# Output projection by seven block products, with weight differences made inside the mLSTM heads

## The chip, the cores and the metric

The kernel runs on one core of a Trainium2 chip. The metric is the device time of one execution in microseconds (us), lower is better. The core has a matrix engine (PE, with its weight loads listed as PEld), a vector engine (DVE), an engine for functions of single elements (ACT), a general one (POOL), and an engine that here only issues transfers between memory and on-chip buffers (SP). Each works through its own instructions in order.

## What is computed

A block with two branches, an mLSTM with four heads and an S5 scan, over x of 1024 rows and 1024 columns in fp32. The branches are merged with gates g, and the merged rows go through one output projection, a norm and a sum with x:

```python
xn = rmsnorm(h, norm_pre_g[l])
proj = xn @ w_in[l]
...
y_a = mlstm_branch(...) @ w_a_out[l]
y_b = s5_branch(...) @ w_b_out[l]
g = jax.nn.sigmoid(g_pre.astype(jnp.float32)).astype(h.dtype)
merged = g[..., :D_MODEL] * y_a + g[..., D_MODEL:] * y_b
h = h + rmsnorm(merged @ w_o[l], norm_post_g[l])
```

`merged`, `w_o` and the product of the two are all 1024x1024. The change is in the last line.

## The kernel before

Every fp32 product is made from three faster ones. A value is split into a high part in the type fp32r and the rest, its low part; `dot3` (L181 to L184) issues high by high (L182), and the two mixed products (L183, L184). So one output bank of 128x512 over k blocks of 128 takes 3k matmuls. Weights come raw into tiles `wr` (two buffers), ACT copies them into `wh` (L142), and DVE or POOL subtracts to give `wl` (L144).

The schedule is written by hand: `tc.manual_schedule()` keeps the order of the code on each engine. The weights stand in a queue filled by `plan`; `fetch` loads the next one (all loads and stores are issued on SP's queue), `pump` splits one and then puts another `fetch` on the list `pending`, `take` hands it to the user. Work comes in units: `run` first empties `pending` (`tick`: this is where stores and fetches reach SP), then does the unit's own loads, then the unit, then those parts of earlier units that were put off by `defer`. `fill` runs the next unit from the list `fillers`.

After the S5 branch and the projections come the four heads. Inside head h stand the attention's own steps (`attn_a` to `attn_e`) and, between them, units of other work: in the first three heads the projections of the next head (`u_unit`, `o_unit`, `z_unit`, `k_unit`, `v_unit`), in the last head the units of the product with `w_a_out` (`ya_unit`), whose weights are loaded in pieces of 256 columns, `("ya", i)`. `o_unit` writes its gate through a tile `sow` with two buffers to scratch memory `so_d` (ACT at L902). `attn_e` splits a head's result: ACT makes the high part, POOL the low part (L1270), and both are stored to `yh_d` and `yl_d`. `ya_unit` stores partial merged rows to `pa_d`, and `ya_pre` loads what it needs, `y_gb<-gb_d` among it (L1296). `load_so` is L1133, all stores by `store` are L82.

The last stage has three kinds of units. `ya_unit(3, ...)`: four of 18 matmuls. `mg_unit(ct, hf)`: sixteen of 6 matmuls of 512 columns, which complete the merged rows ct (of 128) of one half hf of the sequence, in two DVE operations, and split them into `mh` (ACT, L1439) and, one unit later, `ml` (POOL, L1440). `wo_unit(i, t)`: for each of four pieces of 256 columns of `w_o` and each of eight tiles of 128 rows, 24 matmuls of 256 columns into one bank; ACT squares the bank and sums it for the norm (L1460), DVE multiplies it by the gain (L505 under the name ob). With the last piece come the root (POOL, L1467 and L1468), the sum with x (DVE, L1474) and the store.

## Time and profile before

| | |
|---|---|
| three runs | 989.7, 990.56, 987.15 us, median 989.7 |
| the profiled execution | 987.63 us, of which its span is 985.9 |
| PE busy | 972.8 us, 99% of the span, 5644 matmuls |
| DVE, ACT, POOL busy | 621.9 (63%), 352.9 (36%), 207.1 us (21%) |
| granted PE clock, mean | 0.999 of full speed |
| transfers | 145.17 MB, 147 GB/s over the span |

The span is what the trace covers, and the profiled execution's time is 1.7 us longer. Busy time counts an engine's instructions, on PE with pipelined ends that are modelled. An engine that is idle costs nothing by itself: what counts is what PE, or whoever comes last, waits for. In the rows below a timeline's row gives start, duration, engine, line, operation, output and input; "x2" is two instructions in a row, and brackets give the idle time before the row and what ended it.

### The profile page before, as it was taken

Reading aid. Unit: us, or ns where it says so; the run is one execution under the profiler, and the core shown is the slowest. Engines: PE = TensorE matmul, PEld = TensorE weight load, DVE = VectorE, ACT = ScalarE, POOL = GpSimd, SP = SyncE. Lnnn points to the kernel's source line nnn. Section 1 sums busy time; section 2 is a strip of 40 time slices with the busy share of each in tenths; the row PEclk is TensorE's granted clock in tenths of the full one; section 3 lists DMA queues with packets and bytes.
Section 4 is the critical chain, followed back from the end, with each engine's and each line's share of the span. In section 5 each row is a group of like instructions: output and inputs, shape, how many; then the busy total and the mean of one; then the engine's idle time right before and its main releaser. Section 6 shows DMA issues by size and latency. Waiting matters only on the chain.

```text
span 985.9 us, 15233 instructions
## 1 busy us (share of the span) xinstructions
PE 972.8 (99%) x5644; PEld 840.9 (85%) x5644; DVE 621.9 (63%) x1397; ACT 352.9 (36%) x697; POOL 207.1 (21%) x215
## 2 busy tenths in 40 slices
PE   9999999999999999999999999998999999999997
PEld 7888888888887889978998898888988888879997
DVE  5437968879644752444686677747775888664225
ACT  7413132231314421224544445434543452233211
POOL 3013122111112000013111321223222311462002
PEclk9999999999999999999999999999999999999999
DMA  7454323423434566115344254335437895772504
GB/s 257 109 159 150 96 89 99 111 57 110 110 97 166 186 216 229 59 68 148 97 134 152 82 178 124 134 97 177 133 117 226 281 302 191 243 249 90 193 1 172
DMA packets 113722, 145.17 MB, mean 147 GB/s; under 512 B 18888, under 2 KB 71280, under 8 KB 113648
## 3 DMA queue, kind: packets, MB, share of 16 engines
q1 hardware_dynamic: 113648, 144.21, 46.0%
q8 instruction: 44, 0.72, 0.3%
q14 instruction: 30, 0.25, 0.1%
HBM read 98.79 MB, written 45.38 MB: 146 GB/s over the span
## 4 chain that ended last, share of the span: by engine, by line
PE 88%; issue 3%; POOL 3%; DVE 2%; DMA 2%; ACT 1%; SPq 0%; DVEq 0%; POOLq 0%; ACTq 0%
PE pp L182 24%; PE pp L183 23%; PE pp L184 23%; PE pm L184 4%; PE pm L182 4%; PE pm L183 4%; PE pm L1151 1%; POOL wl L144 1%; PE pm L727 1%; PE pm L768 1%; PE pm L767 1%; PE pm L1074 1%; DMA so_d<-sow 1%; POOL ml L1440 1%; POOL t2k L1270 1%
## 5 line engine op out<-in xcount | busy, mean ns | idle before, releaser
L182 PE MATMUL pp<-xh,wh 128*128 128x512 f32 x768 | 306.9, 400 | 0.0
L183 PE MATMUL pp<-xl,wh 128*128 128x512 f32 x768 | 303.8, 396 | 0.0
L184 PE MATMUL pp<-xh,wl 128*128 128x512 f32 x768 | 303.8, 396 | 0.0
L182 PEld LDWEIGHTS pp<-xh,wh 128*128 128x128 f32 x768 | 144.4, 188 | 35.1 <-ACT wt L691 0.8
L184 PEld LDWEIGHTS pp<-xh,wl 128*128 128x128 f32 x768 | 144.4, 188 | 34.6
L183 PEld LDWEIGHTS pp<-xl,wh 128*128 128x128 f32 x768 | 144.5, 188 | 32.4 <-DVE xl L295 0.3
L144 POOL TENSOR_TENSOR wl<-wr,wh 128x1024 fp32r<-128x1024 f32 (+1 forms) x25 | 61.6, 2482 | 229.1 <-ACT wh L142 229.1
L142 ACT ACTIVATE wh<-wr 128x1024 fp32r<-128x1024 f32 (+2 forms) x74 | 71.0, 1006 | 46.5 <-PE pm L183 30.6
L184 PE MATMUL pp<-wh,ml 128*128 128x256 f32 x256 | 72.6, 284 | 1.3 <-POOL ml L1440 1.3
L144 DVE TENSOR_TENSOR wl<-wr,wh 128x1024 fp32r<-128x1024 f32 (+2 forms) x49 | 55.9, 1172 | 27.7 <-ACT wh L142 23.2
L182 PE MATMUL pp<-wh,xh 128*128 128x256 f32 (+1 forms) x256 | 72.3, 282 | 0.6 <-ACT sow L902 0.6
L183 PE MATMUL pp<-wl,mh 128*128 128x256 f32 x256 | 72.5, 283 | 0.0
L182 PE MATMUL pp<-wh,mh 128*128 128x256 f32 x256 | 71.9, 281 | 0.0
L184 PE MATMUL pp<-wh,xl 128*128 128x256 f32 (+1 forms) x256 | 71.8, 281 | 0.0
L183 PE MATMUL pp<-wl,xh 128*128 128x256 f32 (+1 forms) x256 | 71.8, 280 | 0.0
L308 ACT ACTIVATE tg<-pp 128x512 f32<-128x512 f32 x32 | 19.2, 598 | 127.4 <-PE pp L184 89.4
L1048 POOL TENSOR_TENSOR hll<-t2k,hlh 128x512 fp32r<-128x512 f32 x16 | 21.1, 1319 | 182.7 <-ACT hlh L1047 106.0
L184 PEld LDWEIGHTS pp<-wh,ml 128*128 128x128 f32 x256 | 48.1, 188 | 1.7 <-POOL ml L1440 1.7
L182 PEld LDWEIGHTS pp<-wh,mh 128*128 128x128 f32 x256 | 48.7, 190 | 0.5 <-ACT mh L1439 0.4
L182 PEld LDWEIGHTS pp<-wh,xh 128*128 128x128 f32 x256 | 48.1, 188 | 1.2 <-ACT sow L902 1.0
L183 PEld LDWEIGHTS pp<-wl,xh 128*128 128x128 f32 x256 | 48.2, 188 | 0.2
L184 PEld LDWEIGHTS pp<-wh,xl 128*128 128x128 f32 x256 | 48.1, 188 | 0.0
(412 smaller groups left out, 1810.0 us busy)
## 6 DMA issues: line engine op xcount, KB each, us to landing
wr<-in_w_in_dram SPq DMA_DIRECT2D x48, 512.0 KB
t_d<-tg SPq DMA_DIRECT2D x32, 256.0 KB
xt<-in_x_dram SPq DMA_DIRECT2D x8, 512.0 KB
aux<-t_d SPq DMA_DIRECT2D x16, 256.0 KB
gb_d<-aux SPq DMA_DIRECT2D x16, 256.0 KB
so_d<-sow SPq DMA_DIRECT2D x32, 128.0 KB
sz_d<-t2k SPq DMA_DIRECT2D x16, 256.0 KB
cs_d<-t2k SPq DMA_DIRECT2D x16, 256.0 KB
```

The lines of the kernel that those rows point to most:

```text
L142: A.activation(hi, raw, AF.Copy)
L144: eng.tensor_tensor(wl[:, k0:k0 + n, c0:c0 + w], raw, hi.bitcast(F32), op=ALU.subtract)
L182: PE.matmul(o, lh, rh, start=first, stop=False)
L183: PE.matmul(o, lh, rl, start=False, stop=False)
L184: PE.matmul(o, ll, rh, start=False, stop=last)
L308: A.activation(t, o, AF.Tanh, scale=0.5)
L727: PE.matmul(o[NS * b2:NS * (b2 + 1), g * P:(g + 1) * P], q["wt"][:, ri, g, NS * b2:NS * (b2 + 1)], ut[b][:, 2 * g + b2, :], start=True, st ...
L767: PE.matmul(o, m0[:, 2 * g + b2, :], ut[b][:, 2 * g + b2, :], start=True, stop=False)
L768: PE.matmul(o, vs[:, b2, g].rearrange("p t n -> p (t n)"), ss_[:, b2, g, :], start=False, stop=True)
L1048: PL.tensor_tensor(lo, acc, hi.bitcast(F32), op=ALU.subtract)
L1074: PE.matmul(pm[:, 256 * k:256 * k + 256], wt[:, e, 256 + P * k:256 + P * k + P], wt[:, e, 0:256], start=e == 0, stop=e == 1)
L1151: PE.matmul(sc[:, :P], k_[:, m, sl], q_[:, m, sl], start=m == 0, stop=m == 1)
```

## The change

The 1024x1024 product is cut into four blocks of 512 on either side, and made from seven block products instead of eight (in Winograd's form of Strassen's scheme). With A the merged rows and B the weights `w_o`, each product is a sum or difference of A's blocks by a sum or difference of B's:

- p1 = a11 by b11, p2 = a12 by b21, p3 = s4 by b22, p4 = a22 by one combination of the b's, p5 = s1, p6 = s2 and p7 = s3 by three more;
- c11 = p1 + p2, u2 = p1 + p6, u4 = u2 + p5, c22 = u4 + p7, c21 = u2 + p7 + p4, c12 = u4 + p3.

Each product is four units, one bank of 128x512 each, of 4 blocks of k by three matmuls of 512 columns; the last unit of p3 is done in two halves of 256 columns.

**Weights.** The three differences and the fourth combination don't depend on the data, but are made on the chip: `wo_steps`, called in the last `u_unit` of each of the four heads' projections, loads two tiles `wc` with pieces of the four blocks of `w_o` (into the buffers of `wr`), has POOL make four subtractions of 128x256 in each, one and two units later, and four units later stores both to scratch memory `wt_d`. From the call to the stores the list `held` keeps `fetch` from loading the next weights. In the last stage the queue of weights has p1, p2, p6, p5, p7, p4, p3, each 512x512.

**Merged rows and sums.** The low parts are now made by DVE (`al`). When both rows of a pair of the second half are there, `s_pair` makes s3 and s2 by DVE and s1 by POOL; s4 follows later, and the sums are split by ACT and DVE or POOL (`split_1`). The units of ya and mg stand in another order, and the last six mg units stand among those of p1 and p2.

**Ends.** DVE adds each bank to the running sum, ACT squares it, POOL multiplies by the gain (`pmul`), the root is taken on POOL after a DVE sum, and `finish` adds x as before.

Three places of the order are shown. On SP's queue, in the fourth call of `wo_steps`, which comes at the end of the third head; wr is a weight tile of `w_a_out`, xh and xl the rows of y read back, so and y_gb tiles for the head and for ya units. Before:

```order
L1285 DMA xh_97<-yh_d 128x512
L1286 DMA xl_105<-yl_d 128x512
L124 DMA wr<-in_w_a_out_dram 128x4x256
L124 DMA wr<-in_w_a_out_dram 128x2x256
L1133 DMA so<-so_d 128x256 x2
L1294 DMA y_t_7760<-t_d 128x512
L1296 DMA y_gb<-gb_d 128x512
```

and in the changed kernel some 25 transfers later on that queue:

```order
L1336 DMA y_gb<-gb_d 128x512
L1173 DMA so<-so_d 128x256
L83 DMA pa_d<-y_gb 128x512
L1035 DMA wt_d<-wc 128x2x256 x4
L125 DMA wr<-in_w_a_out_dram 128x4x256
L125 DMA wr<-in_w_a_out_dram 128x2x256
L1334 DMA y_t_8113<-t_d 128x512
L1336 DMA y_gb<-gb_d 128x512
L125 DMA wr<-in_w_a_out_dram 128x4x256
L125 DMA wr<-in_w_a_out_dram 128x2x256
```

The load of the second ya piece, which stood ahead of the head's first loads of so, now stands behind the third store of pa_d and the four stores of wt_d, and the third piece's load follows two transfers after it.

On POOL, in the third call, around the low parts of the head's result (L1270 before, L1310 after). Before:

```order
L144 TENSOR_TENSOR wl<-wr,wh 128x1024
L1098 MEMSET vh 128x4
L1099 MEMSET vh 128x4
L1100 MEMSET vl 128x4x2
L1270 TENSOR_TENSOR t2k<-t2k 128x512 x2
L1048 TENSOR_TENSOR hll<-t2k,hlh 128x512
L1050 TENSOR_SCALAR t2k<-t2k,par 128x512
```

and after:

```order
L1140 MEMSET vl 128x4x2
L1026 TENSOR_TENSOR wc<-wc 128x256 x4
L1310 TENSOR_TENSOR t2k<-t2k 128x512 x2
L1026 TENSOR_TENSOR wc<-wc 128x256 x4
L1088 TENSOR_TENSOR hll<-t2k,hlh 128x512
L1090 TENSOR_SCALAR t2k<-t2k,par 128x512
```

Four subtractions of the weights stand ahead of the two of the head's result, and four behind.

On DVE, in the last stage, where the mg units of the second half end. Before (ft and fpa are the rows of mg units, ob those of the output):

```order
L1432 SCALAR_TENSOR_TENSOR ft<-ft,pp 128x512
L505 TENSOR_TENSOR ft<-ft,fpa 128x512
L505 TENSOR_TENSOR ob_9040<-pp,gpo 128x256
L144 TENSOR_TENSOR wl<-wr,wh 128x1024 x2
L505 TENSOR_TENSOR ob_9081<-pp,gpo 128x256
```

and after (r_8701 and r_8702 are rows of the second half and the sums made from them, s2l the low part of s2, a22l that of the block a22, c the sums c11):

```order
L1500 SCALAR_TENSOR_TENSOR r_8702<-r_8702,pp 128x512
L511 TENSOR_TENSOR r_8702<-r_8702,fpa 128x512
L511 TENSOR_TENSOR c_9087<-m_8949,pm 128x512
L511 TENSOR_TENSOR a22l<-r_8702,a22h 128x512
L511 TENSOR_TENSOR r_8701<-r_8693,r_8701 128x512
L511 TENSOR_TENSOR r_8702<-r_8702,r_8701 128x512
L145 TENSOR_TENSOR wl<-wr,wh 128x1024
L511 TENSOR_TENSOR c_9088<-m_8949,pm 128x512
L1520 TENSOR_TENSOR s2l_8886<-r_8702,s2h_8884 128x512
```

Between an mg unit's two operations and the weights for the next product stand the low part, the two differences of the pair and a sum of the output; one half of those weights is DVE's, the other POOL's.

The diff, without the lines that are removed from the last stage and without those helpers of it that the words above describe:

```diff
+    held = []
+
     def fetch():
-        if order and not raw_q:
+        if order and not raw_q and not held:
...
-    for i in range(4):
-        plan(("wo", i), [w_o[0][:, 256 * i:256 * i + 256]], KT, 256)
+    wo11, wo12 = w_o[0][0:512, 0:512], w_o[0][0:512, 512:1024]
+    wo21, wo22 = w_o[0][512:1024, 0:512], w_o[0][512:1024, 512:1024]
+    for n, src in (("p1", wo11), ("p2", wo21), ("p6", wt_d[1, 1]), ("p5", wt_d[0, 0]), ("p7", wt_d[0, 1]),
+                   ("p4", wt_d[1, 0]), ("p3", wo22)):
+        plan(n, [src], 4, 512)
...
+    wsteps = deque((j, q) for j in range(4) for q in range(2))
+
+    def wo_load():
+        j, q = wsteps.popleft()
+        t = wp.tile([P, 2, 2, DH], F32, tag="wr", name="wc")
+        rows = w_o[0].rearrange("(a j p) c -> j p a c", a=2, j=4)[j]
+        for a in range(2):
+            SY.dma_start(t[:, a], rows[:, a].rearrange("p (b c) -> p b c", b=2)[:, :, DH * q:DH * q + DH])
+        return j, q, t
+
+    def wo_comb(j, q, t):
+        sub_ = lambda o, a, b: PL.tensor_tensor(o, a, b, op=ALU.subtract)
+        b11, b12, b21, b22 = t[:, 0, 0], t[:, 0, 1], t[:, 1, 0], t[:, 1, 1]
+        sub_(b11, b12, b11)
+        sub_(b12, b22, b12)
+        sub_(b22, b22, b11)
+        sub_(b21, b21, b22)
+
+    def wo_store(j, q, t):
+        for a in range(2):
+            SY.dma_start(wt_d[a][:, P * j:P * j + P, DH * q:DH * q + DH].rearrange("b p c -> p b c"), t[:, a])
+
+    def wo_steps():
+
+        held.append(1)
+        ts_ = []
+        pending.append(lambda: ts_.extend(wo_load() for _ in range(2)))
+        defer(lambda: wo_comb(*ts_[0]))
+        defer(lambda: wo_comb(*ts_[1]), 2)
+        defer(lambda: pending.extend([lambda: [wo_store(*t) for t in ts_], held.pop, fetch]), 4)
...
         if m and hf:
             pump(pl=True)
+            wo_steps()
...
+            A.activation(ah[b][:, j], t1, AF.Copy)
+            defer(lambda: tt(al[b][:, j], t1, ah[b][:, j].bitcast(F32), ALU.subtract))
+        if hf:
+            pair.setdefault(j, []).append(ct)
+            if len(pair[j]) == 2:
+                defer(lambda: s_pair(j))
...
+    def split_1(n, j, src, eng):
+        h_, l_ = sv[n][0][j], sv[n][1][j]
+        A.activation(h_, src, AF.Copy)
+        return lambda: eng.tensor_tensor(l_, src, h_.bitcast(F32), op=ALU.subtract)
+
+    def s_pair(j):
+
+        a11, a12, a21, a22 = mrow(j, 0), mrow(4 + j, 0), mrow(j, 1), mrow(4 + j, 1)
+        tt(a21, a11, a21, ALU.subtract)
+        tt(a22, a22, a21, ALU.subtract)
+        PL.tensor_tensor(a11, a11, a22, op=ALU.add)
+        defer(split_1(2, j, a22, V))
+        for n, r in ((1, a11), (3, a21), (4, a12)):
+            late_s[n].append((j, r))
+
+    def split_s(n, eng, cnt=1):
+        for j, r in late_s[n][:cnt]:
+            if n == 4:
+                PL.tensor_tensor(r, r, mrow(4 + j, 1), op=ALU.subtract)
+            split_1(n, j, r, eng)()
+        del late_s[n][:cnt]
...
+    def mul_unit(w, lhs, o, tq, cs=slice(0, 512)):
+        hi, lo = lhs
+        sl = slice(tq * P, (tq + 1) * P)
+        for k in range(4):
+            dot3(o, hi[k][:, sl], lo[k][:, sl], *wcur[w](k, cs), k, k == 0, k == 3)
...
+    def wset2():
+
+        fetch()
+        key, _, _, raws = raw_q.popleft()
+        assert key == "p2"
+        h_ = [main.tile([P, 2, 512], F32R, tag=f"xh{4 + k}", name=f"w2h{k}") for k in range(2)]
+        l_ = [main.tile([P, 2, 512], F32R, tag=f"xl{4 + k}", name=f"w2l{k}") for k in range(2)]
+        for i in range(2):
+            raw = raws[i][2]
+            A.activation(h_[i], raw, AF.Copy)
+            PL.tensor_tensor(l_[i], raw, h_[i].bitcast(F32), op=ALU.subtract)
+        wcur[2] = lambda k, cs: (h_[k // 2][:, k % 2, cs], l_[k // 2][:, k % 2, cs])
+        pending.append(fetch)
...
+    def p2(q):
+        if q == 0:
+            c11 = [main.tile([P, 2, 512], F32, tag=f"xh{6 + i}", name=f"c11{i}") for i in range(2)]
+            cb_[0] = [c11[i // 2][:, i % 2] for i in range(4)]
+            hl1 = [block("a1", "s1h", F32R), block("a2", "s1l", F32R)]
+            sv[1] = [rows4(a) for a in hl1]
+        o = mbank()
+        mul_unit(2, (rows4(ah[1]), rows4(al[1])), o, q)
+        tt(cb_[0][q], cb_["m1"][:, q], o, ALU.add)
+        square(cb_[0][q], q, 0)
+        if q == 1:
+            cb_["g"] = main.tile([P, D], F32, tag="xl6", name="gpo")
+            store(cb_["g"], norm_post_g[0].partition_broadcast(P))
+        if q > 1:
+            split_s(1, PL)
+
+    def p6(q):
+        if q == 0:
+            wset(6)
+            cb_["u2"] = block("a3", "u2")
+            y_space(4, 4)
+        o = mbank()
+        mul_unit(6, sv[2], o, q)
+        tt(cb_["u2"][:, q], cb_["m1"][:, q], o, ALU.add)
+        if q == 0:
+            pump()
+        if q < 2:
+            split_s(1, PL)
+        split_s(3, V)
...
+    def p3(q):
+        if q == 0:
+            cb_[1] = rows4(block("a7", "c12"))
+            cb_["raw"] = block("a6", "c12r")
+        n = 1 if q < 3 else 2
+        w = 512 // n
+        o = mbank()
+
+        for i in range(n):
+            cs = slice(w * i, w * i + w)
+            mul_unit(3, sv[4], o[:, cs], q, cs)
+            r = cb_["raw"][:, q, cs]
+            tt(r, cb_["u4"][:, q, cs], o[:, cs], ALU.add)
+            square(r, q, 1 + i)
+            dst = cb_[1][q][:, cs]
+            if n == 1:
+                pmul(dst, r, 512)
+            else:
+                mul(dst, r, cb_["g"][:, 512 + w * i:512 + w * i + w])
+            if i < n - 1:
+                step2()
+                tt(sso[:, q, 3:4], sso[:, q, 3:4], sso[:, q, 1:2], ALU.add)
+        if q < 3:
+            ending(q, n)
+        else:
+            finish(q, rms(q, n))
...
+    def go(f, q):
+        run(unit(lambda: f(q)))
+
+    go(p1, 0)
+    fill(2)
+    for q in range(1, 4):
+        go(p1, q)
+        fill(1)
+        if q == 1:
+            wset2()
+    go(p2, 0)
+    fill(1)
+    go(p2, 1)
+    pump(pl=True)
+    for f, q in [(p2, q) for q in range(2, 4)] + [(f, q) for f in (p6, p5, p7, p4, p3) for q in range(4)]:
+        go(f, q)
+    flush2()
     tick()
 
 

```

## Rows read from the trace of the kernel before

**Rows 1.** The page, part 1: busy us, share of span, instructions by engine.

```profile
PE 972.8 (99%) x5644; PEld 840.9 (85%) x5644; DVE 621.9 (63%) x1397; ACT 352.9 (36%) x697; POOL 207.1 (21%) x215
```

**Rows 2.** Timeline of PE: start us, duration us, engine, line, operation, count.

```profile
99.81 0.39 PE L182 MATMUL pp<-xh,wh 128*128 128x512 f32 x1
122.21 0.39 PE L182 MATMUL pp<-xh,wh 128*128 128x512 f32 x1
...
964.83 0.29 PE L184 MATMUL pp<-wh,ml 128*128 128x256 f32 x1
971.55 0.28 PE L183 MATMUL pp<-wl,mh 128*128 128x256 f32 x1
```

**Rows 3.** Groups of instructions after 740 us: busy us, mean ns | idle.

```profile
L184 PE MATMUL pp<-wh,ml 128*128 128x256 f32 x256 | 72.6, 284 | 1.3 <-POOL ml L1440 1.3
L505 DVE TENSOR_TENSOR ob<-pp,gpo 128x256 f32<-128x256 f32 x32 | 13.6, 424 | 52.7 <-ACT fjk L1460 52.7
```

**Rows 4.** Timeline of PE in the last stage.

```profile
846.23 0.48 PE L182 MATMUL pp<-xh,wh 128*128 128x512 f32 x1
...
883.93 0.39 PE L184 MATMUL pp<-wh,ml 128*128 128x256 f32 x1 [1.06 <-POOL ml L1440]
```

**Rows 5.** The chain that ended last, from 979 us on: start us, us, what.

```profile
979.76 0.13 PE pp L184
...
981.37 0.75 DVE ob L1474
```

**Rows 6.** Timelines of SP, ACT, DVE and PE around the fourth call.

```profile
774.17 0.94 SPq L124 DMA_DIRECT2D wr<-in_w_a_out_dram  x2
...
788.23 0.32 SPq L82 DMA_DIRECT2D pa_d<-y_gb  x1
...
794.56 0.32 SPq L1296 DMA_DIRECT2D y_gb<-gb_d  x1
...
795.45 0.38 SPq L82 DMA_DIRECT2D pa_d<-y_gb  x1
...
797.14 1.58 ACT L142 ACTIVATE wh<-wr 128x1024 fp32r<-128x1024 f32 x2
...
798.23 1.83 DVE L144 TENSOR_TENSOR wl<-wr,wh 128x1024 fp32r<-128x1024 f32 x2 [1.22 <-ACT wh L142]
...
802.75 0.39 PE L182 MATMUL pp<-xh,wh 128*128 128x512 f32 x1
```

**Rows 7.** Stretches: busy us of each engine, PEclk, DMA share, GB/s.

```profile
790.00:795.00 5.00, 5.00 (x34) 4.52 (x33) 4.47 (x10) 2.76 (x9) 1.88 (x2) 1.00 1.02 379
795.00:800.00 5.00, 5.00 (x23) 4.05 (x22) 3.71 (x9) 3.56 (x7) 0.89 (x1) 1.00 0.71 213
```

**Rows 8.** Timelines of SP, ACT, POOL, PE around the second and third call.

```profile
574.76 0.87 SPq L82 DMA_DIRECT2D so_d<-sow  x2
...
577.29 0.39 ACT L902 ACTIVATE sow<-pp 128x256 f32<-128x256 f32 x1 [3.47 <-DMA so_d<-sow]
...
672.94 3.04 POOL L1270 TENSOR_TENSOR t2k<-t2k 128x512 fp32r<-128x512 f32 x2 [3.61 <-DMA wr<-in_w_in_dram]
...
681.95 0.38 ACT L902 ACTIVATE sow<-pp 128x256 f32<-128x256 f32 x1 [5.47 <-DMA so_d<-sow]
...
684.79 0.44 PE L1163 MATMUL pm<-ident,k 128*128 128x128 f32 x2 [2.12 <-DVE ksl L1170]
```

**Rows 9.** Timelines of POOL and DVE in the last head and stage.

```profile
847.49 2.40 POOL L144 TENSOR_TENSOR wl<-wr,wh 128x1024 fp32r<-128x1024 f32 x1 [6.71 <-ACT wh L142]
...
862.82 6.39 POOL L1440 TENSOR_TENSOR ml<-ft,mh 128x512 fp32r<-128x512 f32 x4 [1.29 <-ACT mh L1439]
...
847.75 2.68 DVE L505 TENSOR_TENSOR t2k<-t2k,cz 128x512 f32<-128x512 f32 x1
...
862.71 0.69 DVE L505 TENSOR_TENSOR ft<-ft,fpa 128x512 f32<-128x512 f32 x1
...
864.03 1.08 DVE L505 TENSOR_TENSOR ft<-ft,fpa 128x512 f32<-128x512 f32 x1
```

208 lines of the change are left out of this document (134 added, 74 removed).

## Prediction

> **What bounds the kernel now.** I read the page's busy shares first: TensorE (PE) is busy for 972.8 of the 985.9 us of the span, 99%, and no other engine is over 63% [rows 1]. So time goes only where PE gets less work or stops waiting, and comes only where PE is made to wait. The second reading is therefore PE's own timeline, for the price of one matmul. Two equal matmuls of 512 columns with 96 in all between their starts give (122.21 - 99.81)/96 = 0.2333 us each; two of 256 columns, 56 apart, give (971.55 - 964.83)/56 = 0.120 us [rows 2]. (A record's own duration, 0.39 or 0.29, is longer, since matmuls overlap; the distance of starts is what counts.) The third is the last stage. It begins with the first matmul of the last ya units at 846.23 [rows 4] and ends at 979.76 + 0.13 = 979.89 [rows 5], 133.66 us. It holds 4 ya units of 18 and 16 mg units of 6 matmuls of 512 columns, 168 in all, and 3 x 256 = 768 of 256 columns: one of the three products of the wo units is the group of 256 in [rows 3]. By the prices, 168 x 0.2333 + 768 x 0.120 = 39.2 + 92.2 = 131.4 us. The other 2.3 us are waits; the largest single one, 1.06 us, is for the POOL subtraction that makes ml [rows 4], 1.3 us of such waits in all [rows 3].
>
> **The change, part by part.** *The matmuls.* The 768 go, and seven products of 48 take their place: 324 of 512 columns and 24 of 256, since the last unit of p3 is cut in halves. 324 x 0.2333 + 24 x 0.120 = 75.6 + 2.9 = 78.5 us against 92.2: -13.7. The low parts of the merged rows are now made by DVE, one unit later, and no longer by POOL, so the 2.3 us of waits go too; what may be late instead is priced below. That is **-16.0** for the stage. That it doesn't come out so because the change doesn't do what it says can be left out: PE's order has 420 matmuls fewer, as it should.
>
> These prices can be held against the Trainium skill, "TensorE: Matmul & The Clock Gate", section "Back-to-back issue gap", which gives columns/2.4 + 2.5 ns for one matmul at the full clock: 216 and 109 ns. The rows above show 233 and 120, so trace and page differ; by the page's figures the matmuls would give back 768 x 0.1092 - 324 x 0.2158 - 24 x 0.1092 = 11.3 and the sum below would end at 984.4. I go by the rows.
>
> *The end.* After the last matmul, which starts at 979.76, came ACT's square and two small POOL operations, then DVE's last step at 981.37 [rows 5]. Now DVE first adds u4 to the bank, 256 columns, before ACT can square; DVE's operation on 256 columns from PSUM took 0.42 [rows 3]. With one more hand-over, **+0.5**.
>
> *The sums before the products.* From the first matmul of mg(4,0) to the end of p2 PE has 156 matmuls of 512 columns, 36.4 us. In this stretch DVE now has 41 operations of 128x512 (20 of the ten mg units, 6 low parts, 8 differences of s_pair, 4 low parts of s2, 3 sums c11) at 0.69 when nothing disturbs [rows 9], and three halves of weight splits at about 1.2 (a pair of 1024 and 512 columns took 1.83 [rows 6]): 28.3 + 3.6 = 32 us. POOL has four r11 sums at about 1.5 (two subtractions of the kind took 3.04 [rows 8]) and three weight halves at 2.4 [rows 9]: 13.2 us. Within a stretch of POOL subtractions that lasts 6.39 us the same DVE operation took 1.08 instead of 0.69 [rows 9]; about ten operations meet that: 32 + 10 x 0.39 = 36 us of DVE in 36.4 us of PE. DVE turns from an engine with slack into one without. The wait would fall at p6, the first product that needs the pair sums: the last pair sum, ACT's copy of it, ACT's two copies of p6's weights (1.05 each, two thirds of the 1.58 for 1024 and 512 columns [rows 6]) and POOL's low half (2.40) follow one another and, laid out with these durations, end 0.7 us after PE wants them, and 2.7 if DVE is held as long as in the longest row, the 2.68 of a 0.69 operation [rows 9]. Bounds: 0, if the ten are fewer, and 6, if each of the three POOL weight halves holds DVE by 2.0. I take **+2.0**, near that row.
>
> *Weights for the products.* One product is 48 x 0.2333 = 11.2 us of PE; the next one's weights are split in that time: two copies by ACT, two subtractions by DVE, about 3.5 us with their hand-overs, beside PE. The load of 1 MB has 11.2 - 3.5 = 7.7 us to land. At the 379 GB/s that the queues moved in a full stretch [rows 7] that is 2.8 us: nothing, as long as that cover holds; if it fails, see the slower rival. Evacuation sums, squares and gains come to some 3 operations per unit of 2.8 us on three engines: hidden.
>
> *The pieces in the heads.* Each of four calls loads 1 MB, has POOL make eight subtractions of 128x256 (0.6 to 0.75 each, half of 1.5), stores 1 MB, and holds the weight fetch until the stores are issued. In the first three calls the weights held back still land before they are split, by my reckoning with the rounds below, if only by a few us: nothing, and a wait of the kind of (a) where that is wrong. The gain and the rows of x are loaded a product or more ahead of their use, hidden. Two things are not.
>
> (a) Fourth call, SP's queue. The weights of the second ya column were issued at 774.17 [rows 6], 23 us before ACT copies them at 797.14; DVE subtracts at 798.23, PE uses them from 802.75, and their low part two matmuls later, at 803.2. Now their issue stands behind the four stores, and these behind the third pa_d store, which stood at 795.45 [rows 6]. The load also writes buffers which the stores read. A store's round took 2.5 us at best (574.76 to ACT's release at 577.29 [rows 8]) and 6.3 in a full queue (a store at 788.23, and the load into its tile at 794.56 [rows 6]). Stores at 796 to 797.8, their landing, the load's landing, then 1.05 by ACT and 1.2 by DVE: the low part is there at 804.1 by the short and at 811.7 by the long round, so PE waits 0.9 to 8.5 us. The DMA share falls from 1.02 to 0.71 just there [rows 7], which speaks for the short, though 2 MB more are then under way. I take **+4.0**. Behind the waiting ya matmuls stand the head's own.
>
> (b) Second and third call, POOL. Four subtractions, 2.4 to 3.0 us, stand ahead of the two L1270 operations that make yl; yl's stores are on SP ahead of so_d's, and ACT waits for so_d's to land before it can reuse sow: 3.47 us in one, 5.47 in the other, which ends in 2.12 us of PE waiting [rows 8]. POOL was idle for 3.61 us ahead of its L1270 [rows 8], so the four may fit in: 0. At worst they come whole on the path, less what slack there is, 2 us each: 4. I take 0.8 for the second call, where PE had not waited, and 1.0 for the third: **+1.8**.
>
> *Sum.* -16.0 + 0.5 + 2.0 + 4.0 + 1.8 = -7.7. The profiled execution took 987.63 us with a span of 985.9; the sum gives it 979.9. Against the median of the runs, 989.7, which is what will be compared, it is **982.0**.
>
> **The rivals.** *A: the heads' pieces are hidden.* Short rounds in (a), the four subtractions within POOL's idle time in (b): 5.8 us fewer, -13.5, 976.2. For it: the falling DMA share [rows 7] and the idle time of POOL [rows 8]. Against it: POOL's idle time is needed for two loads to land first, and the queue has 2 MB more. *B: the heads' pieces at their upper ends*: 8.5 + 4 + 2 + 0.5 against 16.0 gives -1.0, 988.7. For it: the 6.3 us round was in this very stretch. Against: (a) and (b) would have to come out badly together.
>
> *C: DVE and POOL block one another for whole operations.* The row with 2.68 us began 0.26 after a POOL subtraction of 2.40 and ended 0.54 after it [rows 9]; if each of the three POOL weight halves does so to DVE, its chain to p6 is 4 us late rather than 2: 984.0. The Trainium skill states this as the rule ("SBUF — State Buffer", section "Who interferes with whom"): an operation of DVE with two SBUF inputs contends with GpSimd for a shared pair, and the loser fully blocks; the row of 2.68 agrees, the row of 1.08 shows less. Against it as a cost: DVE can catch up before p6.
>
> *D, slower than before: weights for the products.* If the loads of wt_d and w_o take 10 us or more from issue to landing, each product from p6 on starts 10 + 3.5 - 11.2 = 2.3 us late, and for five products that is 11.5: -7.7 + 11.5 = +3.8, 993.5. The point from which it costs at all is 7.7 us, and from which it decides 9.3. Against: a load went through in 6.3 us even at a share of 1.02, and the last stage moved less [rows 6, 7].
>
> **How the numbers follow.** The sum's own case 0.46, A 0.25, B 0.16, C 0.08, D 0.05. A difference of 0.3%, 3 us, is about what a measurement of this kernel can tell from no change: faster is below 986.7, slower above 992.7. The sum's case, A and C lie below, and a quarter of B: 0.83. The rest of B, 0.12, is the same, and D, 0.05, slower. The range goes from A with 1.7 us for the scatter of runs, 974.5, to B, 989.0, and leaves D and some of each edge out.
>
> **What would show it.** In the changed profile: matmul starts 0.233 apart in the products; the stage about 118 us and a little, from first ya matmul to last; a PE wait at p6's first matmuls, ended by POOL or DVE; in the fourth call a wait of PE for ACT's wh or DVE's wl of 1 to 8 us, on the ya matmul; in the second and third a longer ACT wait for so_d; some 6.5 us from the last matmul to the end. Wrong would be: PE waits at the start of each product (D), or in the heads at places that I haven't named.

## The result: slower, and where the time went

The changed kernel took 997.88 us in the median of six runs (993.65 to 999.87), the kernel before 988.19 in the median of six; the ratio is 1.0085 with a 95% interval of 1.0058 to 1.0113. Forecast were 982.0 and a range from 974.5 to 989.0; the kernel is slower by 0.9% and lies outside it. The profiled execution took 998.46 us, its span 996.4, against 987.63 and 985.9.

The page's first part of the changed kernel, which answers to [rows 1]:

```profile
PE 966.4 (97%) x5224; PEld 816.4 (82%) x5224; DVE 672.8 (68%) x1432; ACT 364.1 (37%) x689; POOL 255.3 (26%) x253
```

PE has 420 matmuls fewer, as the order said, yet its share of the span fell from 99% to 97% and the span is 10.5 us longer. So PE now waits. The view of waits, PE's own, gives who it waits for (us in total, times, longest):

```profile
PE pm L185 <- DVE c12r L511: 8.2, 1, 8.2
PE pp L185 <- ACT wh L143: 2.5, 1, 2.5
PE pp L185 <- ACT sow L908: 2.1, 2, 1.1
PE pm L1203 <- DVE ksl L1210: 1.9, 1, 1.9
PE pm L187 <- DVE s2l L1520: 1.6, 1, 1.6
```

Before, its longest wait was the 2.12 of [rows 8], which is still there (L1203). The timeline of PE in the changed kernel places the last stage's waits, first the first ya matmul, which answers to 846.23 in [rows 4]:

```profile
855.62 0.47 PE L185 MATMUL pm<-xh,wh 128*128 128x512 f32 x1
...
907.50 0.50 PE L186 MATMUL pm<-w2l,a12h 128*128 128x512 f32 x1 [1.11 <-POOL w2l L1595]
...
919.55 0.49 PE L185 MATMUL pm<-wh,s2h 128*128 128x512 f32 x1 [0.82 <-ACT wh L143]
920.81 0.50 PE L186 MATMUL pm<-wl,s2h 128*128 128x512 f32 x1 [0.77 <-DVE wl L145]
...
923.59 0.80 PE L187 MATMUL pm<-wh,s2l 128*128 128x512 f32 x1 [1.59 <-DVE s2l L1520]
...
987.08 0.58 PE L185 MATMUL pm<-w3h,s4h 128*128 128x256 f32 x1 [8.24 <-DVE c12r L511]
```

So the 10.5 us can be split in three at two points. The last stage starts at 855.62 instead of 846.23: **9.4 us lost before it**. From there to the end of the last matmul, 990.01, it took 134.4 us against 133.7: **the whole gain of the products was lost inside it**. And 6.4 us instead of 6.0 follow after that, as forecast (+0.5).

Inside the stage, 117.7 us of matmuls were forecast. The products ran a little faster than that: from p5's first matmul at 936.23 to that of p4's last unit at 966.25 there are 132 matmuls, 0.2274 us each, against 0.2333 in [rows 2]; that is 1.3 us over p6 to p3. The 16.7 us between 117.7 and 134.4, and this 1.3, went so: 1.1 + 0.8 + 0.8 + 1.6 = 4.3 us in waits at p2 and p6, 8.2 in the last unit, and most of the rest in matmuls that ran at the lower of the clock's two levels (1.2 instead of 2.4 GHz) behind these waits. The stretches show it (length, busy us of PE, PEld, DVE, ACT and POOL with counts, granted clock, DMA share, GB/s; the second and third have PE at p6, the last at the last half unit):

```profile
915.00:920.00 5.00, 4.18 (x18) 2.85 (x16) 3.22 (x6) 3.40 (x6) 1.28 (x1) 1.00 0.00 0
920.00:925.00 5.00, 2.64 (x8) 1.83 (x8) 4.13 (x4) 2.52 (x7) 4.15 (x2) 0.76 0.45 131
925.00:930.00 5.00, 5.00 (x14) 3.90 (x13) 3.01 (x4) 4.07 (x7) 2.36 (x2) 0.56 0.23 82
930.00:935.00 5.00, 5.00 (x23) 4.10 (x23) 4.68 (x5) 1.46 (x3) 5.00 (x4) 1.00 0.65 206
...
985.00:990.00 5.00, 2.92 (x12) 2.63 (x12) 3.88 (x8) 0.51 (x2) 0.97 (x2) 0.50 0.48 179
```

p6's second unit took 3.98 us from start to start where other units took 2.73, its first lost 2.1 besides its waits, and in the last half unit matmuls of 256 columns stood 0.213 apart instead of 0.120: 3.4 + 1.1 = 4.5 us together. 4.3 + 8.2 + 4.5 = 17.0 of 18.0; the last 1.0 us is in small gaps that no row names. The 1.1 at p2 is more than usual: in eleven of the kernels below PE waits 0.3 to 0.6 there.

### The profile page after: what moved, and what is told of

Same layout as the page of the kernel before. It is cut to its first block, busy times and chain, and to the rows that moved or that the text cites. A ratio compares the mean times of both kernels' runs of the same rounds, so it can differ in the third digit from the quotient of the medians.

```text
span 996.4 us, 14515 instructions
## 1 busy us (share of the span) xinstructions
PE 966.4 (97%) x5224; PEld 816.4 (82%) x5224; DVE 672.8 (68%) x1432; ACT 364.1 (37%) x689; POOL 255.3 (26%) x253
## 4 chain that ended last, share of the span: by engine, by line
PE 77%; DMA 8%; DVE 6%; issue 4%; ACT 2%; POOL 2%; SPq 0%; DVEq 0%; POOLq 0%; ACTq 0%
PE pp L185 19%; PE pp L187 18%; PE pp L186 18%; PE pm L187 5%; PE pm L185 5%; PE pm L186 5%; DMA xh<-yh_d 1%; DMA so_d<-sow 1%; PE pm L1191 1%; DVE c L1567 1%; DVE r L511 1%; DMA wt_d<-wc 1%; ACT wh L143 1%; DMA r<-t_d 1%; PE pm L733 1%
## 5 line engine op out<-in xcount | busy, mean ns | idle before, releaser
L185 PE MATMUL pp<-xh,wh 128*128 128x512 f32 x736 | 294.0, 399 | 2.5 <-ACT wh L143 2.5
L187 PE MATMUL pp<-xh,wl 128*128 128x512 f32 x736 | 291.1, 395 | 0.5 <-DVE wl L145 0.5
L186 PE MATMUL pp<-xl,wh 128*128 128x512 f32 x736 | 291.0, 395 | 0.0
L185 PEld LDWEIGHTS pp<-xh,wh 128*128 128x128 f32 x736 | 138.3, 188 | 36.1 <-ACT wh L143 2.7
L187 PEld LDWEIGHTS pp<-xh,wl 128*128 128x128 f32 x736 | 138.2, 188 | 34.3 <-DVE wl L145 1.0
L186 PEld LDWEIGHTS pp<-xl,wh 128*128 128x128 f32 x736 | 138.4, 188 | 31.2 <-DVE xl L301 0.3
L314 ACT ACTIVATE tg<-pp 128x512 f32<-128x512 f32 x32 | 19.2, 599 | 127.4 <-PE pp L187 89.4
L1068 DVE SCALAR_TENSOR_TENSOR t2k<-pp,par,t2k 128x511 f32<-128x511 f32 (+2 forms) x48 | 35.7, 744 | 5.1 <-ACT t2k L1061 4.6
L1244 ACT ACTIVATE cth<-ct 128x516 fp32r<-128x516 f32 x28 | 17.8, 637 | 54.9 <-DVE ct L1234 48.4
L1164 POOL TENSOR_TENSOR q<-hlh,hll 128x512 f32<-128x512 f32 x16 | 21.2, 1349 | 46.7 <-DVE q L511 36.6
L511 DVE TENSOR_TENSOR sTl<-sT,sTh 128x128 fp32r<-128x128 f32 x32 | 21.1, 658 | 16.8 <-ACT sTh L1199 16.2
```

What stands on the lines that cost most here:

```text
L185: PE.matmul(o, lh, rh, start=first, stop=False)
L186: PE.matmul(o, lh, rl, start=False, stop=False)
L187: PE.matmul(o, ll, rh, start=False, stop=last)
L314: A.activation(t, o, AF.Tanh, scale=0.5)
L511: V.tensor_tensor(o, a, b, op=op)
L1068: V.scalar_tensor_tensor(acc[:, s:], o[:, :512 - s], cw[:, j, ct:ct + 1], acc[:, s:], op0=ALU.mult, op1=ALU.add)
```

## The experiments

Each time is compared with the changed kernel's 997.88 and the kernel before, which ran beside it each time at 987.7 to 988.7. "Stage" is the time from the last stage's first matmul to the end of the span: 139.7 before, 140.8 in the changed kernel. This and the start of the stage tell the three places apart better than the median does, since the changed kernel's own runs scatter over 6 us and some 1.1 us of its profiled execution were lost by 334 us, ahead of every edit. Three tries below that left the wait in the last unit at 7.6 to 8.0 us still came out at 994.3 to 995.4. So some 3 us of a difference to the changed kernel's median need not be the edit's, and what an edit did is read from its trace.

### The heads: pieces left out, moved, three calls of four, subtractions later

**Without the pieces.**

```diff
-    for n, src in (("p1", wo11), ("p2", wo21), ("p6", wt_d[1, 1]), ("p5", wt_d[0, 0]), ("p7", wt_d[0, 1]),
-                   ("p4", wt_d[1, 0]), ("p3", wo22)):
+    for n, src in (("p1", wo11), ("p2", wo21), ("p6", wo12), ("p5", wo11), ("p7", wo21),
+                   ("p4", wo22), ("p3", wo22)):
...
             pump(pl=True)
-            wo_steps()
```

> The changed kernel without the weight pieces in the heads: no loads, subtractions or stores there, no held fetch, and p6, p5, p7, p4 take plain blocks of w_o instead of differences (so this run computes another product). Theory (the pieces cost what the trace shows in the heads): the first ya matmul of the last stage, at 855.62 in the changed kernel and 846.23 in the one before, comes back to 847 or below, and the time falls by 8 to 9.5 us. Rival (part of those 9.4 us lies outside the pieces, in the 1.4 us that had been lost by 334 us, before any head): it comes to 848 and the time falls by 7 to 8. The wait of 8.2 us in the last unit stays under both.

986.7 us (ratio to before 0.9973 to 0.9991), 11.2 below the changed kernel. The stage starts at 846.85: 8.8 us earlier. Its own length, 139.1, hardly changes, and the last unit still waits 7.4. The pieces cost what the trace showed; the part outside them is small.

**Three calls of four.**

```diff
             pump(pl=True)
-            wo_steps()
+            if h < H - 1:
+                wo_steps()
```

> The changed kernel with the pieces in the first three calls only, and plain blocks of w_o in p6, p5, p7, p4 (another product). Theory (step (a) as predicted: the fourth call costs what PE waits for the late fetch, 2.5 + 0.5 and what follows): the last stage starts 3.5 to 4.5 us earlier than with four calls, the rest of the 8.8 us stays. Rival (the calls share one cause, and the third one's delays and the lower clock behind them make most): 1 to 2 us earlier.

990.87 us. The stage starts at 849.54, 6.1 earlier than with four calls, and 2.7 later than without pieces. The profiled executions of the eight kernels that keep all four calls as they are start it at 852.3 to 855.6, so by the starts the fourth call is worth 3 to 6 us, which holds the expected 3.5 to 4.5 but tells no more. Matched by their order with those of the kernel before, PE's matmuls tell it within one execution: over the fourth call they fall 3.2 to 4.9 us further behind in the nine traces that have it, and 0.0 in this one. That is the step as predicted, and the trace of the changed kernel shows the mechanism. SP, ACT, DVE and PE in the fourth call, to be read against [rows 6]:

```profile
801.70 0.38 SPq L83 DMA_DIRECT2D pa_d<-y_gb  x1
802.13 2.83 SPq L1035 DMA_DIRECT2D wt_d<-wc  x4
806.04 1.68 SPq L125 DMA_DIRECT2D wr<-in_w_a_out_dram  x2
```

```profile
809.77 1.58 ACT L143 ACTIVATE wh<-wr 128x1024 fp32r<-128x1024 f32 x2 [4.75 <-DMA wr<-in_w_a_out_dram]
```

```profile
810.86 1.83 DVE L145 TENSOR_TENSOR wl<-wr,wh 128x1024 fp32r<-128x1024 f32 x2 [6.08 <-ACT wh L143]
```

```profile
810.88 0.50 PE L185 MATMUL pp<-xh,wh 128*128 128x512 f32 x1 [2.48 <-ACT wh L143]
...
812.14 0.50 PE L187 MATMUL pp<-xh,wl 128*128 128x512 f32 x1 [0.53 <-DVE wl L145]
```

The load went out at 806.04 behind the third pa_d store (801.70) and the four stores (802.13), ACT copied at 809.77, and PE waited 2.48 for the high and 0.53 for the low part. Matched by their order, PE's matmuls there go from 5.5 us behind the kernel before to 9.4 behind: 3.9 us, where 4.0 had been taken.

**Subtractions later.**

```diff
-        defer(lambda: wo_comb(*ts_[0]))
-        defer(lambda: wo_comb(*ts_[1]), 2)
+        defer(lambda: wo_comb(*ts_[0]), 2)
+        defer(lambda: wo_comb(*ts_[1]), 3)
```

> The changed kernel with POOL's subtractions of the pieces one unit later in each call, behind the low parts of the head's result. Theory (step (b): the subtractions ahead of those low parts delay yl's stores, the so_d stores behind them and ACT's reuse of sow): PE's two waits for sow fall from 1.0 and 1.1 us to the 0.3 of the kernel before. Rival (the sow stores are late for the four loads of the pieces on SP's queue and engines): they stay at 1.

994.79 us in its profiled execution, its only run. The waits for sow in the second call, of the changed kernel (PE, then ACT) and of this one (PE, then ACT):

```profile
573.73 0.38 PE L185 MATMUL pp<-wh,xh 128*128 128x256 f32 x1 [0.97 <-ACT sow L908]
```

```profile
595.06 0.38 ACT L908 ACTIVATE sow<-pp 128x256 f32<-128x256 f32 x1 [4.73 <-DMA so_d<-sow]
```

```profile
571.96 0.39 PE L185 MATMUL pp<-wh,xh 128*128 128x256 f32 x1 [0.32 <-ACT sow L908]
```

```profile
593.67 0.38 ACT L908 ACTIVATE sow<-pp 128x256 f32<-128x256 f32 x1 [5.03 <-DMA so_d<-sow]
```

PE's waits for sow in the second and third call fall from 0.97 and 1.15 to 0.32 each, the value before: POOL's subtractions ahead of yl were their cause. But ACT's second wait, 4.73 us at 595.06, stays at 5.03, and the kernel before has none there. By the order on SP's queue it belongs there: behind the piece's stores (579.87) and the weight load that they held (586.64) the sow stores are issued late; no run tests this by itself. PE pays for it with 0.44 us before the head's q and k matmuls at 599.03, and by 606 it has fallen 1.4 us further behind the kernel before. That half of (b) hadn't been predicted.

**Pieces in the first stages.** The same work through a buffer of its own, in sixteen pieces of half the width, one step every unit from the fifth unit on, and no `held` (a piece has four steps, so it comes every four units and not every five):

```diff
+        t = gp_.tile([P, 2, 2, wcol], F32, tag="wc", bufs=1, name="wc")
...
+            SY.dma_start(t[:, a], rows[:, a].rearrange("p (b c) -> p b c", b=2)[:, :, cs])
+        yield
+        yield
+        sub_(b11, b12, b11)
...
     def run(u):
         tick()
+        ncall[0] += 1
+        if wo_gen and ncall[0] > 4:
+            next(wo_gen[0], None)
```

> The changed kernel with the weight pieces made in the first stages instead of the heads: sixteen pieces of half the width through one buffer of their own, a load, four POOL subtractions of 128x128 and a store every five units from the fifth unit on; no held fetch. Theory (the heads' pieces cost by what they delay there: fetch, POOL, the sow stores): the last stage starts at 847 instead of 855.6 and the time falls by 8 to 10 us, as without the pieces. Rival (the same transfers and subtractions cost PE time wherever they stand): it falls by less than 4.

994.23 us, 3.7 below the changed kernel: the rival's number, under 4, but not for its reason. The last pieces ran into the first head, where the constants bif then stood behind a piece's store on SP's queue, and PE had a new wait (view of waits):

```profile
PE pp L185 <- DVE gall L547: 3.1, 1, 3.1
```

With the lower clock behind it this left PE 5.7 us behind the changed kernel at 402 us. From there on PE gained 8.6 us on it: the stage starts at 852.71. So the pieces were free in the first stages but not this far on; in the combined versions below they have three steps and come every three units, end well before the heads, and the stage starts at 846.9 to 849.1.

### The end: what makes DVE late in p4 and p3

The last unit's wait is for DVE's reading of the first half of its bank (c12r). DVE in p3 of the changed kernel (c12r is the sum from the bank, fs the sum for the root, c<-c,fs,xr the two finishing operations of an earlier row), and POOL's gain in the same time:

```profile
976.93 0.67 DVE L511 TENSOR_TENSOR c12r<-u,pm 128x512 f32<-128x512 f32 x1
977.67 2.51 DVE L1567 SCALAR_TENSOR_TENSOR c<-c,fs,xr 128x512 f32<-128x512 f32 x2
980.10 0.15 DVE L511 TENSOR_TENSOR fs<-sso 128x1 f32<-128x1 f32 x1
980.17 0.68 DVE L511 TENSOR_TENSOR c12r<-u,pm 128x512 f32<-128x512 f32 x1
980.98 2.43 DVE L1567 SCALAR_TENSOR_TENSOR c<-c,fs,xr 128x512 f32<-128x512 f32 x2
```

```profile
977.68 1.28 POOL L1611 TENSOR_TENSOR c<-c12r,gpo 128x512 f32<-128x512 f32 x1
...
980.93 1.27 POOL L1611 TENSOR_TENSOR c<-c12r,gpo 128x512 f32<-128x512 f32 x1
```

One unit of DVE lasts 3.24 us (from 976.93 to 980.17) against 2.76 of PE, and 2.4 to 2.5 of it are the two finishing operations. Undisturbed, a DVE operation of this size takes 0.69 [rows 9], two 1.4. Two explanations stood against one another: **P**, POOL's gain holds DVE, and **L**, DVE lost 4.8 us at p7's end (p7's last bank was complete at 958.26, its sum came at 963.08) while it waited for p3's weights and split them; such a lag of a sum behind its bank is called DVE's debt below.

**Without gains.**

```diff
-        pmul(c, c, 0)
...
-                pmul(dst, r, 512)
+                cb_[1][q] = r
```

> The changed kernel with POOL's multiplications by the gain left out in p4 and in the first three units of p3 (so part of the output lacks the gain). Theory P (POOL's operation holds DVE's finishing pair, 2.43 us instead of 1.42): the pairs fall to 1.4, DVE needs 2.4 us per unit of 2.8 and catches up, PE's wait in the last unit falls from 8.2 to under 2 and the time by 6 to 8 us. Rival L (the debt is the 4.8 us that DVE lost at the end of p7, where it waited for the weights of p3, and stays): the wait falls to 4 or 5, the time by 3 to 4.

986.45 us (0.9968 to 0.9993), and the wait is 1.1. DVE now:

```profile
967.32 0.69 DVE L511 TENSOR_TENSOR c12r<-u,pm 128x512 f32<-128x512 f32 x1
967.92 1.41 DVE L1567 SCALAR_TENSOR_TENSOR c<-c,fs,xr 128x512 f32<-128x512 f32 x2
969.25 0.15 DVE L511 TENSOR_TENSOR fs<-sso 128x1 f32<-128x1 f32 x1
970.09 0.69 DVE L511 TENSOR_TENSOR c12r<-u,pm 128x512 f32<-128x512 f32 x1 [0.68 <-PE pm L187]
```

Two finishing operations take 1.41, DVE waits for PE (0.68), and the stage is 130.4. That is what P expected, although this run can't tell whether POOL's operation holds DVE's or only delays the root, which POOL makes too; the next tries can.

**p3's weights later.**

```diff
-        if q == 2:
-            wset3()
...
+        if q == 1:
+            wset3()
```

> The changed kernel with the split of p3's weights put in p4's second unit instead of p7's third, where DVE waited for their load. Theory L (the debt is the wait for that load): p7's last sum, at 963.08, comes at 959, and the wait in the last unit falls from 8.2 to about 4, the time by 4 us. Theory P alone (DVE's finishing pairs set the end): the same work is only moved, DVE is as late at the end, and the time stays within 1.5 us.

995.27 us. p7's last sum came at 955.34 for a bank complete at 955.30, so the debt there was gone, and the wait is 8.0 all the same; the stage, 139.2, is 1.6 shorter. L alone falls. (The split's 2.6 us now lay in p4, so the debt was partly moved.)

**Finishing through PSUM, first and second try.** ACT multiplies by the root into a PSUM bank and DVE adds x, so DVE's operation has one SBUF input; in the second try begun a unit later, and with the small sum for the root on POOL:

```diff
-            V.scalar_tensor_tensor(c, c, s, xres[t][:, qs_], op0=ALU.mult, op1=ALU.add)
+            y = bank()
+            A.activation(y, c, AF.Copy, scale=s)
+            tt(c, y, xres[t][:, qs_], ALU.add)
```

> The changed kernel with the finishing step in two: ACT multiplies the row by its root into a PSUM bank, DVE adds x to that bank, so that DVE's operation has one SBUF input only; POOL's gains stay. Theory P: DVE's operation takes 0.7 each whether POOL works or not, the wait in the last unit falls under 2 and the time by 5 to 8 us. Rival L: as in the run without gains, the wait falls to 4 or 5. Rival (ACT becomes late instead): ACT has 0.8 for the square and 2 x 0.6 per unit of 2.8, the wait is then for ACT and the time falls by less than 3.

> The changed kernel with the finishing step through PSUM (ACT by the root, DVE adds x) begun two units after its row's sum and ahead of that unit's own work, and with the small sum for the root on POOL. In the run that only split the step, DVE's operations fell to 0.65 each but DVE waited 1.4 us per unit for ACT, whose multiplication stood behind the square of the same unit's sum. Theory (DVE's time per unit, operations and hand-overs, sets the end): now 2.1 us per unit of 2.8, the wait of 8.2 in the last unit falls under 1 and the time by 8 to 10 us. Rival (the debt of p7's end stays): the wait falls to 4 or 5, the time by 4.

995.39 and 994.28 us, waits of 7.6 and 7.7: both missed. The second try's DVE shows why:

```profile
974.03 0.68 DVE L511 TENSOR_TENSOR c12r<-u,pm 128x512 f32<-128x512 f32 x1
976.14 1.38 DVE L511 TENSOR_TENSOR c<-pp,xr 128x512 f32<-128x512 f32 x2 [1.43 <-ACT pp L1568]
```

Two operations now take 1.38 beside POOL's gain, as theory P says, but DVE waits 1.43 for ACT: on ACT the multiplication stands behind the square of the sum that DVE has just made. The unit lasts 3.40 (974.03 to 977.43). What counts is DVE's whole period, its operations and its waits.

**Third try.** ACT's multiplications (`finish_a`) ahead of a unit's own work, DVE's additions (`finish_b`) behind it, and the small sum for the root on POOL as in the second try:

```diff
         early.append(lambda: s_.append(rms(t, i)))
-        defer(lambda: finish(t, s_[0]))
+        defer(lambda: early.append(lambda: finish_a(t, s_[0])))
+        defer(lambda: finish_b(t), 2)
```

> The changed kernel with the finishing step through PSUM, this time ACT's two multiplications ahead of a unit's own work and DVE's two additions behind it, so that DVE doesn't wait for ACT; small root sum on POOL. Theory (what sets the end is DVE's period per unit, operations held by POOL or hand-overs, 3.25 us before, 3.3 in the two earlier tries, against 2.76 of PE): now about 2.1 us, the debt of 4 to 5 us at p7's end is paid back in eight units, the wait of 7 to 8 us falls to under 1.5 and the time by 7 to 10 us, as in the run without gains. Rival (any DVE debt at p7's end stays): the wait is still 4 or more.

986.69 us (0.9973 to 0.9995), 11.2 below the changed kernel, the wait 0.9, the stage 130.9:

```profile
970.80 0.69 DVE L511 TENSOR_TENSOR c12r<-u,pm 128x512 f32<-128x512 f32 x1 [0.88 <-PE pm L187]
971.41 1.28 DVE L511 TENSOR_TENSOR c<-pp,xr 128x512 f32<-128x512 f32 x2
```

DVE waits for PE in each unit. The debt of p7's end was there as in the changed kernel (its sum at 958.34 for a bank complete at 954.35) and was paid back. The last unit took 4.15 us instead of 12.74, and the steps after PE's last matmul 0.6 more. Shown, then: with its period of 3.25 us, made by POOL's gain, DVE couldn't pay a debt back but added to it. Of the 8.2 us, 4.8 stood at p7's end and 3.4 came after. The debt counts by itself where it is larger: in one version below (DVE making both halves of p6's weights) it was 8.9 us, and with the new end 4.1 were still left in the last unit.

**The last unit in one piece.**

```diff
-        n = 1 if q < 3 else 2
+        n = 1
```

> The changed kernel with the last unit of p3 in one piece of 512 columns. Theory (PE's wait of 8.2 us in front of the second half shows DVE's debt: the half's bank is free only when DVE has read the first half): the wait disappears from PE, but the sums, roots and additions of the last units still come as late on DVE, and the time falls only by the 2 to 3 us that PE's second half and its sum took behind them. Rival (the half's bank is the cause by itself): the time falls by 7 or more.

992.02 us, 5.9 lower, and the stage 136.6, 4.1 shorter. By that it lies between the two expectations, but only what follows the start of p3's last unit is the edit's: 16.1 us to the end of the span instead of 19.1, 3.0 shorter and so the theory's 2 to 3. PE's wait is gone and its last matmul ends at 977.21, but the span ends 13.2 us later. The chain that ended last has no PE from 970 us on (shares of that stretch by line):

```profile
by line: DVE c L1567 38.0%; issue 13.6%; POOL fs L1560 7.6%; DVE fs L511 7.5%; DVEq L1787 3.0%; ACT junk L1555 2.9%; DVE c12r L511 2.8%; POOLq L1787 2.7%; ACTq L1787 0.5%; DVE sso L1695 0.3%; POOLq L1560 0.2%; ACTq L1555 0.1%
```

PE's wait was DVE's debt at another place. That the half waited for the other half's reader still cost these 3 us of its own, since its matmuls came behind the wait and at the lower clock.

### Before p6: POOL's operations hold DVE's

**Without the sums of s1.**

```diff
-        PL.tensor_tensor(a11, a11, a22, op=ALU.add)
```

> The changed kernel without POOL's four sums of s_pair (s1 is then a11, so the product is another one). Theory C (POOL's operations hold DVE's in the stretch before p6): DVE has its sums ready 3 to 4 us earlier, the waits of 3.2 us at p6 and the stretch at the lower clock behind them go, the time falls by 3 to 5 us. Rival (p6 waits for its weights: ACT's copies, begun after p2's second unit, and the subtractions after them): the 1.6 us for wh and wl stay, the time falls by 1.6 or less.

990.49 us, the stage 134.0, 6.8 shorter than in the changed kernel. The waits for w2l, wh and wl are gone (2.7 us) and with them the lower clock at p6, but the 1.6 us for s2's low part stay. From the stage's first matmul to p5's first it takes 74.5 us, where the changed kernel took 80.6 and eleven other kernels with these sums 78.5 to 79.7: the sums cost 4 to 6 us there, C's 3 to 5 or a little more, though one of the waits that C named is left. POOL's sums made the weights late; the row for s2 has another cause. In the changed kernel, POOL's half of p6's weights and DVE's s2l:

```profile
920.52 2.47 POOL L145 TENSOR_TENSOR wl<-wr,wh 128x1024 fp32r<-128x1024 f32 x1 [1.28 <-ACT wh L143]
```

```profile
921.27 2.27 DVE L1520 TENSOR_TENSOR s2l<-r,s2h 128x512 fp32r<-128x512 f32 x1
```

and in two versions from below, which differ in this alone, one with that half on POOL and one where DVE makes both halves:

```profile
909.05 2.27 DVE L1523 TENSOR_TENSOR s2l<-r,s2h 128x512 fp32r<-128x512 f32 x1
```

```profile
913.42 0.69 DVE L1523 TENSOR_TENSOR s2l<-r,s2h 128x512 fp32r<-128x512 f32 x1
```

### A version from the findings

Three edits together: the early pieces every three units, the third try's end, and POOL's sums of s1 made beside their splits (from p2's last unit on).

> A version from the three findings: the pieces in the first stages (every four units, so that they end before the heads' constants are loaded), the end as in the run with ACT ahead and DVE behind, and POOL's four sums of s1 made only in p2's last unit and p6, where s1 is split. If the three causes are the ones found and add up: -8 in the heads, -8 at the end, -3 to -5 before p6, so 976 to 981. If a cause only moves (POOL's later sums delay p5, or the early pieces the first stages), 983 or more.

982.34 us (0.9920 to 0.9954 of the kernel before). At p6 PE waits for s2's low part as before and no longer for the weights; new is a wait at p5, for s1, 3.1 us with two shorter ones:

```profile
913.05 0.50 PE L187 MATMUL pm<-wh,s2l 128*128 128x512 f32 x1 [1.60 <-DVE s2l L1523]
...
926.83 0.50 PE L185 MATMUL pm<-wh,s1h 128*128 128x512 f32 x1 [1.84 <-ACT s1h L1522]
```

So the third edit had moved a wait. Two attempts to place it better, and the other two edits alone:

> The version from the three findings, with POOL's four sums of s1 beside their splits in p2's third and fourth unit and p6's first two, one unit earlier than there. In that version PE waited 3.1 us at p5 for s1 (ACT's copy and POOL's low part, made last in p6) beside 1.6 us for s2 at p6. Theory (that wait is the sums put too late): the 3.1 us at p5 go, the 1.6 at p6 stay, the time falls by 2 to 4 us. Rival (POOL's work beside the pair sums costs at p6 what it saves at p5): the wait at p6 grows to 3 or more and the time stays within 1 us.

> The same, and both halves of p6's low weights on DVE instead of one on POOL. Theory C (DVE's last low part of s2, 2.27 us instead of 0.68, is held by POOL's half of the weights): the operation falls to 0.7, the second half costs DVE 1.2, and the wait of 1.6 at p6 falls to about 1. Rival (POOL's sums of s1, now first in its queue, hold it as long): it stays at 1.6 or grows.

> The pieces in the first stages and the new end, with POOL's sums of s1 left where the change had them. From the last stage's first matmul to the end of the span the run with the end alone took 130.9 us, the three versions with the sums moved took 132.0 to 133.9. Theory (moving the sums only moved the wait, to p5, and paid nothing): 847 to 848.5 for the start of the stage + 130.9 + 1.8 = 980 to 981, 1 to 2 us below those versions, with 3 us of waits at p6 and none at p5. Rival (it paid 3 us or more): 985 or more.

982.44 and 982.17 us: the waits at p5 came to 2.8 and 2.0, so POOL's sums cost there what they no longer cost at p6. From the stage's first matmul to p7's first the three versions took 91.5, 90.6 and 88.5 us and the two edits alone 89.4: only the last placement gained anything, 0.8 us. With POOL's half of the weights gone the 2.27 us of s2l became 0.69, as the row above shows, and the wait at p6 for it 1.1 instead of 1.6, but PE then waited 0.8 for DVE's second half. The profiled execution of this version, the slowest of its four (980.49 to 984.83), also lost 4.1 us in the last unit, since p3's weights came late (p7's last bank was complete at 948.72):

```profile
956.42 1.23 DVE L1616 TENSOR_TENSOR w3l<-wr,w3h 128x1024 fp32r<-128x1024 f32 x1 [3.11 <-ACT w3h L1615]
957.57 0.68 DVE L546 TENSOR_TENSOR c<-u,pm 128x512 f32<-128x512 f32 x1
```

```profile
PE pm L185 <- DVE c12r L546: 4.1, 1, 4.1
```

Whether it would be the best without that isn't shown. **Two edits alone gave 980.07 us (0.9905 to 0.9938)**, as expected; the stage takes 130.7 from 847.70. This version beats both kernels, the one before by 7.7 us in the same comparison and the changed one's median by 17.8. It still waits 3.2 us at p6.

## Why the prediction was wrong

Forecast and span lie 18.2 us apart (-7.7 and +10.5): 9.3 at the end, 5.7 before p6, 2.4 in (b), 1.1 ahead of every edit and 1.0 in small gaps, less 1.3 for the matmuls' pace.

- **The matmuls, -13.7 in a sum of -16.0: right.** Pace 0.2274 where 0.2333 was taken; the count as ordered. In the last version most of it shows. The sentence on the Trainium skill ("TensorE: Matmul & The Clock Gate", "Back-to-back issue gap") gave 0.216 for 512 columns: the changed kernel's rows stay above it too.
- **Evacuation in p4 and p3: the step that failed.** "Some 3 operations per unit of 2.8 us on three engines: hidden" counted operations by engine without writing DVE's own list: the sum, two finishing operations and two small ones, 0.68 + 1.42 + 0.3 = 2.4 us when undisturbed, against 2.76. That leaves 0.4, and POOL's gain, 1.3 us in each unit, was known from the text itself to stretch a DVE operation. The prediction applied this to the sums before p6 and not here. It cost 8.2 us of PE and 1.1 at the lower clock behind them: without gains the last unit took 4.35 us and with the third end 4.15, instead of 12.74. (Their stages are 10 us shorter, but 2 of these lie before p5, where nothing was edited.) The split of the weights, which the prediction put "beside PE", has a part in it: among DVE's operations that of p3's made 4.8 us of the debt.
- **The sums before p6: the mechanism right, 4.3 us in place of 2.0, and a clock not thought of.** 3.2 of the 4.3 came at p6 and 1.1 at p2. Rival C had priced 4; with the slower matmuls behind them the waits cost 7.7 us. Rival C's cause is shown for s2's low part, by the row of 2.27 us that became 0.69, and for the weights by the run without POOL's sums. The rule of the Trainium skill ("SBUF — State Buffer", "Who interferes with whom"), that of two such operations one fully blocks, agrees: DVE's s2l began at 921.27 and ended at 923.54, 0.55 after POOL's operation of 920.52 to 922.99.
- **(a), the fourth call: right**, 3.9 against 4.0. (Its 804.1 and 811.7 start from the middle of the four stores; from the last, at 797.8, they would be 805.1 and 812.7. The 4.0 lies between in both.)
- **(b): right for what it named** (0.65 + 0.85 us against 1.8), but the same calls delayed the sow stores on SP's queue a second time (1.4), and the third call's two waits, 1.15 and 1.92, were followed by a stretch at the lower clock, 1.3 us: 4.2 in all, where 4 had been the upper bound. That the calls made the 1.3 isn't shown: three versions without pieces in the heads have such a stretch at the same place, and five kernels with both waits have none (last section).
- **The end, +0.5: right**, 6.4 against 6.0. (The last matmul before starts at 979.60; 979.76 is the start of the chain's last piece of it.)
- **The rivals.** What came is none of them: slower, as D said, but not by D's weights; PE didn't wait at the start of p5, p7, p4 or p3. B's 988.7 had 12.5 us in the heads, where the pieces cost 8.1, and missed the end of the kernel. The range held only ends that the sum had named, and no price for an unnamed wait or for the clock behind one.

## What to carry to other kernels

When work per PE unit shrinks, write for each other engine the list of its operations in one unit, with hand-overs, and compare the period with PE's: an engine at 87% of it has no room for a neighbour that holds its operations. A cost that is taken out of one stretch must be looked for in the next one that reads the same data; PE's view of waits, run by run, shows whether it went or moved. Work that no product waits for yet (here differences of weights) belongs where its engine and its queue have nothing due soon.

## What the runs showed of the hardware

- Behind waits PE's matmuls ran at the lower of the clock's two levels, 1.2 GHz, in some executions and not in others. At p6, waits of 2.4 to 3.2 us together were followed by it in all twelve traces that have them (a granted clock of 0.76 and 0.56 in the two stretches above), and a single wait of 1.6 us there in none of three. The 2.2 to 3.0 us of the fourth call were followed by it in five of nine traces and not in the changed kernel's. In the third head a wait of 1.0 to 1.3 us and one of 1.6 to 1.9 were followed by it in three of eight, a single longer wait of 1.7 to 2.2 us in four of eight: not in the kernel before, whose PE waited 2.12 us at 684.79, but in the best version with nearly the same wait. So the length of the waits alone doesn't tell it. The kernel before, and then that version's wait and stretch:

```profile
685.00:690.00 5.00, 4.79 (x40) 4.61 (x39) 4.74 (x18) 2.42 (x7) 0.00 (x0) 1.00 0.31 109
```

```profile
685.14 0.44 PE L1206 MATMUL pm<-ident,k 128*128 128x128 f32 x2 [2.11 <-DVE ksl L1213]
```

```profile
685.00:690.00 5.00, 4.86 (x27) 4.72 (x28) 4.75 (x18) 2.50 (x8) 0.24 (x1) 0.66 0.30 105
```

- A small DVE operation with two SBUF inputs is held as long as a large one: the sum for the root on 128x1 elements (fs), 0.15 us by itself, took 1.25 at 972.51 and 975.75 while POOL's gain ran. That gain had begun during a finishing operation of DVE and itself took 1.74 instead of 1.28:

```profile
975.25 1.74 POOL L1611 TENSOR_TENSOR c<-c,gpo 128x512 f32<-128x512 f32 x1 [0.86 <-ACT junk L1555]
975.75 1.25 DVE L511 TENSOR_TENSOR fs<-sso 128x1 f32<-128x1 f32 x1
```

- The addition of x with one input in PSUM was never held: in the seven traces that have it each took 0.67 to 0.69, two 1.28 to 1.38, beside POOL's gain too, against 2.43 to 2.51 for two finishing operations with both tensors in SBUF (1.41 where the gain was left out).
